# The sample's half of the last projection, from channels on the partitions to tokens on the partitions

## The chip, the core and the metric

The kernel runs on one core of one Trainium2 chip. The metric is the device time of one execution in microseconds (us), as the median of several runs. TensorE multiplies matrices, VectorE and ScalarE work on tiles of 128 partitions, SyncE (SP) issues most transfers and ScalarE's queue (ACT) some.

## The reference

A hybrid encoder layer: one big input projection, three branches (S5, GLA, RG-LRU), a gated sum of their outputs, an output projection, the residual and a final norm. There is one prompt of 512 tokens and one sample of 256; both go through the same layer with 2048 channels. What the change touches is the end:

```python
m = gates[:, :, 0] * (y_a @ w_out_a) + gates[:, :, 1] * (y_b @ w_out_b) + gates[:, :, 2] * (y_c @ w_out_c)
z = z + m @ w_o                                   # w_o: 2048 x 2048
y = z * rsqrt(mean(z * z, axis=-1) + 1e-6) * final_norm_g
```

Inputs and outputs are float32. Each operand is split into an upper and a lower part (hi, lo); a product is hi x hi + hi x lo + lo x hi, three matmuls.

## The kernel before

Tiles hold channels on the 128 partitions and tokens in the columns. Everything here happens in `merge_and_project`. Program order gives the order of each engine's instructions to a scheduler that may move them as far as the buffers allow; on the chip each engine runs its own fixed list.

The prompt's loop goes over eight pairs of column tiles of w_o (p), four steps each (sb). A step's weights come as four quarters B12, B11, B21, B22 in one load of 512 KB (`fetch`, `quarter_weights`, L1205 is the load). The tile `raw` has two buffers. ScalarE casts three of the quarters to `hi` (128x768, L88), VectorE subtracts to get `lo` (L60); `weight_sums` puts the four sums T1 to T4 into `t`, which has one buffer, with three VectorE instructions (`t<-raw` 128x512, then two of 128x256); then `t` is split the same way (128x1024). `hi` and `lo` have three buffers each, and a step takes two of each. `products` (L1144) runs seven products by Winograd's form, 42 matmuls of 256 columns per step: the products 1, 2 and 3 take the split quarters, then 6, 7, 5 and 4, of which the first three and the last take the split sums.

Behind the products of each step stand 12 matmuls of the sample (`sample_mm`, L1417): the quarters B11 and B21 are plain columns of w_o, so they serve as stationary weights while the sample's 256 tokens move. After four steps `combine` takes the seven products from PSUM and adds them to the residual (one ScalarE copy and 11 VectorE instructions of 128x256), and the sample's tile is added and written to the scratch tensor `zspill`. The squares of the prompt's previous pair (`square`) run on ScalarE and are summed on VectorE in the loop.

The tail does the sample's other eight column tiles: three loads per tile (`fetch_last`, 384 or 320 KB, L1472), their split, 48 matmuls of 256 columns (L1417). Between these splits stand the prompt's norm (`prompt_norm`, a matmul with a matrix of ones, L1493) and the 16 scalings and output transfers of the prompt (`prompt_out`). The sample's norm goes across partitions by a matmul with ones (L1542), and eight products of 128x512 with eight transfers of 256 KB end the kernel (L1548).

Of the kernel before, what the change touches and what calls it, by code (L numbers as in the profile page):

```python
# [30 lines left out]
PN = (1, 2)  # L31
# [63 lines left out]
def build(tc, A, out_p, out_s):  # L95
# [11 lines left out]
    zspill = drm.tile([8, 128, NS], F32, name="zspill")  # L107
    xnorm = drm.tile([16, 128, NT], F32, name="xnorm")

# [103 lines left out]
    def proj(ci, n0):  # L213
        """column tile ci of w_in against the activations; two PSUM banks of T/2 or NT/2 tokens"""
# [10 lines left out]
    def evac(dst, ps, n0, func=AF.Copy, scale=1.0):  # L225
        """dst (AP [128, T or NT]) = func(ps * scale)"""
# [14 lines left out]
    # merge tiles piecewise, between the steps of a branch that keeps the vector engine busy: rate microseconds of the  # L241
    # tensor engine for one of the vector engine
# [37 lines left out]
    def cover(n):  # L280
        """n steps"""
# [10 lines left out]
    def flush():  # L292
        """no tile is left half done"""
# [5 lines left out]
    # the first u tiles: two with the contraction outermost, so that they run while x arrives, and a third and the  # L299
    # low-rank gate before the norms are there  # L300
# [41 lines left out]
    # rows 0..31 carry the upper parts of the gate's weights, rows 32..63 the lower ones  # L342
# [6 lines left out]
    # u, cut into chunks of 8 tokens: ud[channel, token of the chunk, chunk]  # L349
# [20 lines left out]
    # the activations get their norm  # L370
# [37 lines left out]
def branch_s5(E):  # L408
# [4 lines left out]
    NG, L, NQ, NE = 32, 8, T // 8, 8     # groups, chunk, chunks, eighths of the groups  # L413
# [56 lines left out]
    # quadrant bits of n1: n1 = 4 m + 2 b2 + b1  # L470
# [22 lines left out]
    # f = (A - 1) / lambda  # L493
# [8 lines left out]
    TT(n1, n1, r, mul)                      # re f  # L502
# [26 lines left out]
    # A^8 for the rows of the scan: backwards twice, forwards twice  # L529
# [11 lines left out]
    def coef(tab, base, kstep, k0, nk):  # L541
        """[128, 4 groups, nk, 16] view of table entries, power k0 + kstep * slot"""
# [4 lines left out]
    # chunk inputs X = E^T U into W  # L547
# [54 lines left out]
    # outputs: within the chunk (T), from the states before it and after it  # L602
    def within(e):
# [3 lines left out]
        for d in range(2):  # L607
# [10 lines left out]
            # B with its factor f; the fifth group is only there to fill 32 columns  # L618
# [65 lines left out]
    # skip, gelu, glu, gate; tokens in the order (token of the chunk, chunk)  # L684
# [58 lines left out]
def branch_gla(E):  # L743
# [42 lines left out]
    for hp in range(2):  # L786
        # cumulated log gates, restarted in every block of 128 tokens
# [27 lines left out]
        # v by tokens: [token, block, (head of the pair, dv)], block 0 the meta tokens  # L815
# [19 lines left out]
        # states before each block  # L835
# [49 lines left out]
        # blocks  # L885
# [39 lines left out]
        # norm over dv, with the next projections between  # L925
# [28 lines left out]
def exp_acc(V, out, x, r, k, ki):  # L954
    """out = exp(x), to the last bits; 0 and inf outside of float32's range; r, k and ki are places for the parts"""
# [13 lines left out]
def lru_rates(V, col, cst, gp):  # L969
    # c = -8 softplus(-lam)  # L970
# [23 lines left out]
def branch_lru(E, first, cp, cn):  # L994
# [8 lines left out]
    def load_half(ci, hk):  # L1003
        """the weights run a half tile ahead"""
# [18 lines left out]
    def conv(n, ps):  # L1023
        """the convolution of channel tile n, and the weights of its gates"""
# [22 lines left out]
    # the functions of a pair of channel tiles by the tables that they need  # L1047
# [16 lines left out]
    def decays(n, gate):  # L1064
        out = []
        for d in range(2):
# [4 lines left out]
            # 1 - a^2 = tanh(-log a) (1 + a^2)  # L1071
# [55 lines left out]
def weight_sums(V, r, t):  # L1127
    """r: B12, B11, B21, B22; t: T1, T3, T2, T4"""
# [6 lines left out]
def products(PE, ps, ws, sb, n, operand, nt=HN):  # L1135
    """two of the n steps of the seven products' contraction, for nt tokens of either half"""
# [31 lines left out]
def merge_and_project(E, yh, yl, out_p, out_s):  # L1168
    """the sum of the gated branch outputs, its projection, the residual and the final norm, channels on the partitions.
    The third branch goes by Winograd's form, the others as they are, for some column tiles before it and for the rest  # L1170
    behind it. The projection of the prompt goes by Winograd's form too. The sample's goes as it is, with the weights
    that are there for the prompt for the first column tile of every pair, and behind the prompt for the second."""
# [13 lines left out]
    def slot(n, dt=F32):  # L1186
        """one of the 28 places of a tile of all tokens, m0 to m15 and c0 to c11"""
# [33 lines left out]
    def fetch():  # L1221
        """the weights of the step after those that are there"""
# [75 lines left out]
    def third(p):  # L1298
# [11 lines left out]
        for e in range(2):  # L1310
# [3 lines left out]
            else:  # L1314
                # no place is left for whole gates
# [35 lines left out]
    def whole(k):  # L1351
        """an operand that both the prompt and the sample take as it is"""
# [32 lines left out]
    def z_pieces(j):  # L1385
        """the place of a channel tile of the prompt's output: (AP, first token, tokens)"""
# [14 lines left out]
    rest = {}  # L1401

    def rest_tile():
        if not rest:
            rest["m7"] = slot("m7")
        return rest["m7"]

    def square(j, h):
        """the squares of half a channel tile, added to the sum"""
        sq, acc = z_tile(10)[:, ss], rest_tile()[:, h * HP:(h + 1) * HP]  # L1410
        S.activation(out=acc if j == 0 else sq, in_=z_halves(j)[h], func=AF.Square)
        return lambda: j and TT(acc, acc, sq, add)
# [6 lines left out]
    def sample_add(po, z):  # L1419
        TT(z, po[:, :NS], z, add)  # L1420

    zsp = E["zspill"]
    for p in range(8):
        ps = seven()
        po = next_bank()
        for sb in range(4):
            if p:
                later = square(2 * (p - 1) + sb // 2, sb % 2)
            ws = ahead.pop(0)
            products(PE, ps, ws, sb, 8, out_operand, HP)  # L1430
            for kk in range(2):
                for i in range(2):
                    # B11, then B21
                    sample_mm(po, [x[:, i] for x in ws[:2]], kk, 2 * sb + kk + 8 * i, sb == kk == i == 0,
                              sb == 3 and kk == i == 1)
            fetch()
            if p:
                later()
            if sb == 2:
                for j in (2 * p, 2 * p + 1):  # L1440
                    residual(j)
                zs = rest_tile()[:, ss]
# [348 lines left out]
```

## Time and profile before

| | |
|---|---|
| runs | 2052.61, 2052.55, 2051.8 us; median 2052.55 |
| profiled execution | span 2048.7 us from its first to its last instruction; no time of its own beside that is given, and the median lies 3.85 us above the span |
| TensorE, weight loads | 2012.0 us (98%), 1983.8 us (97%) |
| VectorE, ScalarE | 1477.2 us (72%), 798.3 us (39%) |
| prompt's loop | first product 1781.67, last sample matmuls end 1989.0 |
| tail | 1989.0 to 2035.5, then 13.3 us to the end |

A row of a timeline gives the start, the duration, the engine, the line and the operation as "written tile <- read tiles"; in brackets stands how long the engine was idle before it, and what released it. The duration of a matmul is longer than the distance to the next one, because they overlap; what a matmul costs in a stream is that distance. For VectorE too, the next instruction may start before the one ahead has ended. Granted clock 1.00 is 2.4 GHz.

### The profile page before, as it was taken

The page shows a single profiled execution, that of the slowest core. Times are in us where ns is not written, and L with a number is a line of the kernel's source. Part 1 is how long each engine was busy: PE and PEld are TensorE (multiplying, and loading weights), DVE is VectorE, ACT ScalarE, POOL GpSimd, SP SyncE. Part 2 cuts the span into 40 slices and gives each one's busy share as a digit, 9 for nine tenths or more (in the row PEclk, how much of TensorE's full clock was granted, in tenths as well). Part 3 has the DMA queues.
Part 4 walks back from the last instruction along what each step waited for, and adds up shares of the span by engine and source line. Part 5 has one row for each costly group of instructions (what it writes and reads, how often), then busy time and mean ns, then how long its engine had stood idle before and what let it go on. Part 6 is the DMA issues. An engine that isn't in the chain of part 4 may idle for free.

```text
span 2048.7 us, 30974 instructions
## 1 busy us (share of the span) xinstructions
PE 2012.0 (98%) x12276; PEld 1983.8 (97%) x12276; DVE 1477.2 (72%) x2738; ACT 798.3 (39%) x1162; POOL 0.2 (0%) x4
## 2 busy tenths in 40 slices
PE   8999989999999999999999999999999999999997
PEld 8999989999998999999999999999999999999997
DVE  8988982634565678687776566656668988887778
ACT  7332111423343677543333222222235435533345
POOL 0000000000000000000000000000000000000000
PEclk9999999999999999999999999999999999999999
DMA  8752134422011222253333222222256335532246
GB/s 291 253 119 95 73 100 126 143 74 74 33 69 40 68 77 75 91 195 124 134 134 111 88 103 103 103 88 103 103 173 223 124 105 182 173 126 93 93 160 219
DMA packets 104225, 248.97 MB, mean 122 GB/s; under 512 B 18832, under 2 KB 39824, under 8 KB 104080
## 3 DMA queue, kind: packets, MB, share of 16 engines
q1 hardware_dynamic: 76496, 199.04, 29.1%
q10 hardware_dynamic: 27584, 47.96, 6.6%
q8 instruction: 96, 1.57, 0.3%
q14 instruction: 49, 0.40, 0.1%
HBM read 199.07 MB, written 47.88 MB: 121 GB/s over the span
## 4 chain that ended last, share of the span: by engine, by line
PE 83%; DVE 10%; ACT 3%; DMA 2%; issue 1%; SPq 0%; ACTq 0%; DVEq 0%
PE br L1144 22%; PE pm L1144 21%; PE pm L198 16%; PE pm L272 8%; PE pm L1417 4%; DVE sc L60 2%; DMA c<-gspill 2%; DVE W L60 2%; PE pm L331 2%; DVE lo L60 1%; PE br L1287 1%; PE pm L1287 1%; PE br L1057 1%; DVE m L60 1%; PE br L198 1%; PE br L1417 1%
## 5 line engine op out<-in xcount | busy, mean ns | idle before, releaser
L88 ACT ACTIVATE hi<-raw 128x768 fp32r<-128x768 f32 (+2 forms) x234 | 217.6, 930 | 526.6 <-PE pm L198 135.2
L60 DVE TENSOR_TENSOR lo<-raw,hi 128x768 fp32r<-128x768 f32 (+2 forms) x234 | 248.1, 1061 | 168.5 <-ACT hi L88 168.4
L60 DVE TENSOR_TENSOR lo<-t,hi 128x1024 fp32r<-128x1024 f32 x132 | 161.6, 1224 | 184.0 <-ACT hi L88 183.8
L88 ACT ACTIVATE hi<-t 128x1024 fp32r<-128x1024 f32 x132 | 139.9, 1060 | 265.1 <-PE br L1144 133.8
L198 PE MATMUL pm<-h,hi 128*128 128x392 f32 (+1 forms) x736 | 195.8, 344 | 1.2 <-ACT xp L1026 1.2
L198 PE MATMUL pm<-h,lo 128*128 128x392 f32 (+1 forms) x736 | 192.4, 341 | 2.5 <-DVE lo L60 2.5
L198 PE MATMUL pm<-l,hi 128*128 128x392 f32 (+1 forms) x736 | 192.9, 341 | 0.0
L1144 PE MATMUL br<-l,hi 128*128 128x384 f32 (+1 forms) x592 | 189.1, 319 | 0.0
L1144 PE MATMUL br<-h,lo 128*128 128x384 f32 (+1 forms) x592 | 188.5, 318 | 0.0
L1144 PE MATMUL br<-h,hi 128*128 128x384 f32 (+1 forms) x592 | 188.5, 318 | 0.0
L1144 PE MATMUL pm<-l,hi 128*128 128x384 f32 (+1 forms) x464 | 153.5, 331 | 0.1
L1144 PE MATMUL pm<-h,lo 128*128 128x384 f32 (+1 forms) x464 | 152.4, 328 | 0.0
L1144 PE MATMUL pm<-h,hi 128*128 128x384 f32 (+1 forms) x464 | 152.4, 328 | 0.0
L198 PEld LDWEIGHTS pm<-h,lo 128*128 128x128 f32 x736 | 134.9, 188 | 2.8 <-DVE lo L60 2.8
L198 PEld LDWEIGHTS pm<-h,hi 128*128 128x128 f32 x736 | 134.9, 189 | 2.8 <-ACT xp L1026 1.5
L198 PEld LDWEIGHTS pm<-l,hi 128*128 128x128 f32 x736 | 134.4, 189 | 0.2
L272 PE MATMUL pm<-h,lo 128*128 128x384 f32 x512 | 131.2, 337 | 2.0 <-DVE lo L60 2.0
L272 PE MATMUL pm<-h,hi 128*128 128x384 f32 x512 | 133.1, 341 | 0.0
L272 PE MATMUL pm<-l,hi 128*128 128x384 f32 x512 | 131.8, 338 | 0.0
L1144 PEld LDWEIGHTS br<-h,lo 128*128 128x128 f32 x592 | 111.5, 188 | 0.0
L1144 PEld LDWEIGHTS br<-h,hi 128*128 128x128 f32 x592 | 111.2, 188 | 0.2 <-ACT h L88 0.2
L1144 PEld LDWEIGHTS br<-l,hi 128*128 128x128 f32 x592 | 111.2, 188 | 0.0
(361 smaller groups left out, 4681.0 us busy)
## 6 DMA issues: line engine op xcount, KB each, us to landing
raw<-in_w_st SPq DMA_DIRECT2D x84, 512.0 KB
raw<-in_w_in SPq DMA_DIRECT2D x82, 512.0 KB
gspill<-g ACTq DMA_DIRECT2D x48, 384.0 KB
raw<-in_w_ost SPq DMA_DIRECT2D x32, 512.0 KB
xr<-in_xT SPq DMA_DIRECT2D x31, 392.0 KB
m<-gspill SPq DMA_DIRECT2D x26, 384.0 KB
raw<-in_w_out SPq DMA_DIRECT2D x16, 512.0 KB
raw<-in_w_outc SPq DMA_DIRECT2D x16, 512.0 KB
```

What stands on the lines that cost most here:

```text
L60: return f(*a, **k)
L88: ins = self.eng.activation(**k)
L198: PE.matmul(ps[h][:, :nw], w[:, k, :], xx[kt][:, n0 + h * nw:n0 + (h + 1) * nw], start=(kt == 0 and j == 0), stop=(kt == 15 and j == 2))
L272: PE.matmul(ps[h][:, :HN], w[:, k % 8, :], xx[k][:, NM + h * HN:NM + (h + 1) * HN], start=(k == 0 and j == 0), stop=(k == 15 and j == 2))
L331: PE.matmul(ps0[2 * t + h][:, :HT], w[:, k, :], xx[kt][:, h * HT:(h + 1) * HT], start=(kt == 0 and j == 0), stop=(kt == 15 and j == 2))
L1057: PE.matmul(ps[:, :HC], w[:, gs], xx[:, sl], start=(j == 0), stop=(j == 2))
L1144: PE.matmul(ps[j][:, :nt], w[:, wi, kk, :], x, start=(k == 0 and q == 0), stop=(k == n - 1 and q == 2))
L1287: PE.matmul(ps[h][:, :HN], w[:, 4 * b + k, :], yy[4 * b + k][:, h * HN:(h + 1) * HN], start=(k == 0 and j == 0), stop=(k == 3 and j == 2))
L1417: PE.matmul(po[:, :NS], x[:, n, :], y[k][:, ss], start=(first and j == 0), stop=(last and j == 2))
```

## The change

The sample's matmuls leave the loop: a step has 42 matmuls. `zspill` is gone. After the loop the whole sample product is made in the tail with the operands' roles exchanged: 128 tokens of the sample are the stationary operand, 512 output columns of w_o move. The tail has four chunks of 512 columns (c), in each of them eight units (u) of two contraction tiles; a unit is a load of 512 KB, a split, and six matmuls of 512 columns for either half of the tokens (t = 0, 1). All of w_o is loaded a second time for it, 32 x 512 KB, into the two buffers of `raw`, the one of `t`, and two half tiles, in turn. The first units' loads are issued in the last pair of the loop.

The residual and the final gain for the tokens' layout are loaded from new inputs (`load_chunk`, 16 transfers on ScalarE's queue, 3 MB). The squares of the prompt leave the loop and run at two tiles per unit from the first unit; the prompt's norm and its outputs follow. The sample's sum of squares is made along the row by ScalarE (`accum_out`), one column per chunk, so that the norm is one number per partition; no matmul with ones is needed. In the last chunk the second half of the tokens runs one unit behind the first, so that the first half's norm and outputs run beside its last matmuls. The output of the sample is [256, 2048], in eight transfers of 256 KB.

```diff
-    def sample_mm(po, w, n, k, first, last):
-        hi, lo = w
-        for j, (x, y) in enumerate(((hi, mh), (hi, ml), (lo, mh))):
-            PE.matmul(po[:, :NS], x[:, n, :], y[k][:, ss], start=(first and j == 0), stop=(last and j == 2))
+    def load_unit():
+        c, u = units.pop(0)
+        n = raws[0]
+        raws[0] += 1
+        if n % 4 < 3:
+            r = (bp.tile([128, 2, 512], F32, name="t") if n % 4 == 2 else
+                 wp.tile([128, 2, 512], F32, name="raw", bufs=2))
+            SP.dma_start(r[:], A["w_os"][c, :, 2 * u:2 * u + 2, :])
...
+    def split_unit():
+        if loaded:
+            hi = wp.tile([128, 2, 512], F32R, name="hi")
+            lo = wp.tile([128, 2, 512], F32R, name="lo")
+            for kk, r in loaded.pop(0):
+                split(hi[:, kk], lo[:, kk], r)
+            wq.append((hi, lo))
     for p in range(8):
         ps = seven()
-        po = next_bank()
         for sb in range(4):
-            if p:
-                later = square(2 * (p - 1) + sb // 2, sb % 2)
             ws = ahead.pop(0)
             products(PE, ps, ws, sb, 8, out_operand, HP)
-            for kk in range(2):
-                for i in range(2):
-                    sample_mm(po, [x[:, i] for x in ws[:2]], kk, 2 * sb + kk + 8 * i, sb == kk == i == 0,
-                              sb == 3 and kk == i == 1)
             fetch()
-            if p:
-                later()
+            if p == 7 and sb > 0:
+                load_unit()
...
+        if p == 7:
+            split_unit()
         combine(V, S, ps, u2, u3, z_halves(2 * p), z_halves(2 * p + 1), u4)
-        sample_add(po, zs)
-        SP.dma_start(zsp[p], zs)
+    def load_chunk(c):
+        for t in range(2):
+            S.dma_start(zc[c][t][:, pp], A["xs"][t, :, c * 512:(c + 1) * 512])
+            S.dma_start(zc[c][t][:, ss], A["g_row"][:, c * 512 + t * NS:c * 512 + (t + 1) * NS].to_broadcast([128, NS]))
+    def chunk_done(c, t, po):
+        z = zc[c][t][:, pp]
+        TT(z, po[:], z, add)
+        sq = bu.tile([128, NT], F32, name="u")[:, pp]
+        S.activation(out=sq, in_=z, func=AF.Square, accum_out=s_(t, c))
+        if c < 3:
+            for h in range(2):
+                TT(z[:, h * NS:(h + 1) * NS], z[:, h * NS:(h + 1) * NS], zc[c][h][:, ss], mult)
...
+    def unit_mm(po, w, t, u):
+        for kk in range(2):
+            k = 2 * u + kk
+            ts = slice(NP_ + t * 128, NP_ + (t + 1) * 128)
+            for q, (x, y) in enumerate(((mh, w[0]), (ml, w[0]), (mh, w[1]))):
+                PE.matmul(po[:], x[k][:, ts], y[:, kk], start=(k == 0 and q == 0), stop=(k == 15 and q == 2))
+    for c in range(4):
+        po = [next_bank() for t in range(2)]
+        held = None
+        for u in range(8):
+            if c == 0 and u < 4:
+                load_chunk(u)
+            w = wq.pop(0)
+            unit_mm(po[0], w, 0, u)
+            if c < 3:
+                unit_mm(po[1], w, 1, u)
+            elif held:
+                unit_mm(po[1], held, 1, u - 1)
+            held = w
+            load_unit()
+            split_unit()
+            for j in range(2):
+                if n < 16:
+                    prompt_square(n)
+                    n += 1
+                    if n == 16:
+                        prompt_norm()
+                        break
+            else:
+                if n == 16 and outs:
+                    prompt_out(outs.pop(0))
+        if c == 3:
+            chunk_done(3, 0, po[0])
+            sample_out(0)
+            unit_mm(po[1], held, 1, 7)
+            chunk_done(3, 1, po[1])
+            sample_out(1)
+        else:
+            for t in range(2):
+                chunk_done(c, t, po[t])
```

How the change moves instructions is seen in the engines' fixed lists; a name such as c_16486 is a place in SBUF, m_16528 the tile `m7`, which before holds the sum of squares and the sample's place, u the scratch of combine, pm and br PSUM banks.

VectorE between the last step of one pair and the second step of the next, from one split of sums (`lo<-t,hi`) to the following one. Before:

```order
L60 TENSOR_TENSOR lo<-t,hi 128x1024
L60 TENSOR_TENSOR u<-br,u 128x256
L60 TENSOR_TENSOR m_16528<-pm,m_16528 128x256
L60 TENSOR_TENSOR m_17779<-m_17779,u 128x256
L60 TENSOR_TENSOR lo<-raw,hi 128x768
L60 TENSOR_TENSOR u<-u,br 128x256
L60 TENSOR_TENSOR t<-raw 128x512
L60 TENSOR_TENSOR m_17470<-m_17470,u 128x256
L60 TENSOR_TENSOR t<-raw,t 128x256
L60 TENSOR_TENSOR t<-t,raw 128x256
L60 TENSOR_TENSOR m_16528<-m_16528,m_16644 128x256
L60 TENSOR_TENSOR lo<-t,hi 128x1024
```

After, at the same place:

```order
L59 TENSOR_TENSOR lo<-t,hi 128x1024
L59 TENSOR_TENSOR u<-pm,u 128x256
L59 TENSOR_TENSOR lo<-raw,hi 128x768
L59 TENSOR_TENSOR m_17998<-m_17998,u 128x256
L59 TENSOR_TENSOR t<-raw 128x512
L59 TENSOR_TENSOR u<-pm,u 128x256
L59 TENSOR_TENSOR t<-raw,t 128x256
L59 TENSOR_TENSOR m_17998<-m_17998,u 128x256
L59 TENSOR_TENSOR t<-t,raw 128x256
L59 TENSOR_TENSOR u<-u,pm 128x256
L59 TENSOR_TENSOR m_17997<-m_17997,u 128x256
L59 TENSOR_TENSOR lo<-t,hi 128x1024
```

The sample's addition (`m_16528<-pm`) and the squares' sum are gone; of combine's instructions four stand ahead of the last sum of `t`, as before. In the round ahead of this one two of them do (`u<-pm,u` and `m_17997<-m_17997,u`), also as before.

VectorE in the tail, where the prompt's scalings (`SCALAR_TENSOR_TENSOR` with `small`) stand among the splits. Before:

```order
L60 TENSOR_TENSOR lo<-m_18997,hi 128x640
L60 SCALAR_TENSOR_TENSOR c_16524<-c_16524,small,m_18786 128x512
L60 SCALAR_TENSOR_TENSOR c_16525<-c_16525,small,m_18786 128x512
L60 SCALAR_TENSOR_TENSOR c_16524<-c_16524,small,m_18786 128x256
L60 SCALAR_TENSOR_TENSOR c_16525<-c_16525,small,m_18786 128x256
L60 TENSOR_TENSOR c_18778<-pm,c_18778 128x256
L60 SCALAR_TENSOR_TENSOR c_16855<-c_16855,small,m_18786 128x512
L60 TENSOR_TENSOR lo<-m_19020,hi 128x640
L60 TENSOR_TENSOR c_18784<-c_18784 128x256
L60 SCALAR_TENSOR_TENSOR m_16856<-m_16856,small,m_18786 128x512
L60 TENSOR_TENSOR lo<-m_19043,hi 128x768
L60 SCALAR_TENSOR_TENSOR c_16855<-c_16855,small,m_18786 128x256
```

After, the last of the scalings ahead of the split of unit 17 (the addition `c_18316<-pm` of chunk 1 and two scalings stand ahead of these rows, the split of unit 16 is nine rows above that addition):

```order
L59 SCALAR_TENSOR_TENSOR c_16486<-c_16486,small,m_18323 128x256
L59 SCALAR_TENSOR_TENSOR c_16487<-c_16487,small,m_18323 128x256
L59 SCALAR_TENSOR_TENSOR c_16759<-c_16759,small,m_18323 128x512
L59 SCALAR_TENSOR_TENSOR m_16760<-m_16760,small,m_18323 128x512
L59 SCALAR_TENSOR_TENSOR c_16759<-c_16759,small,m_18323 128x256
L59 SCALAR_TENSOR_TENSOR m_16760<-m_16760,small,m_18323 128x256
L59 SCALAR_TENSOR_TENSOR m_17253<-m_17253,small,m_18323 128x512
L59 SCALAR_TENSOR_TENSOR m_17254<-m_17254,small,m_18323 128x512
L59 TENSOR_TENSOR c_18316<-c_18316 128x256
L59 TENSOR_TENSOR c_18316<-c_18316,c_18317 128x256
L59 TENSOR_TENSOR c_18317<-pm,c_18317 128x512
L59 TENSOR_TENSOR lo<-raw,hi 128x1024
```

Before, a split follows after at most five scalings; after, ten scalings, the chunk's products and both its additions stand ahead of the next split.

ScalarE at the end of the loop; `in_xs` and `in_g_row` are the new inputs, `hi<-t` and `hi<-raw` casts of the last steps of the loop and of the first unit:

```order
L87 ACTIVATE hi<-t 128x1024
L87 ACTIVATE hi<-raw 128x768
L1464 DMA c_18316<-in_g_row 128x256
L1463 DMA c_18317<-in_xs 128x512
L1464 DMA c_18317<-in_g_row 128x256
L1463 DMA c_18319<-in_xs 128x512
L1463 DMA c_18318<-in_xs 128x512
L87 ACTIVATE hi<-t 128x1024
L1464 DMA c_18318<-in_g_row 128x256
L1464 DMA c_18319<-in_g_row 128x256
L1463 DMA c_18320<-in_xs 128x512
L1464 DMA c_18320<-in_g_row 128x256
```

Before there was no transfer on ScalarE's queue here; now 16 stand among the last casts of the loop, and each waits on ScalarE's queue for its place.

## Rows read from the trace of the kernel before

**Rows 1.** Page: busy time and instructions by engine, chain by engine

```profile
PE 2012.0 (98%) x12276; PEld 1983.8 (97%) x12276; DVE 1477.2 (72%) x2738; ACT 798.3 (39%) x1162; POOL 0.2 (0%) x4
...
PE 83%; DVE 10%; ACT 3%; DMA 2%; issue 1%; SPq 0%; ACTq 0%; DVEq 0%
```

**Rows 2.** Windows: length, busy PE PEld DVE ACT POOL, PEclk, DMA share, GB/s

```profile
1680.00:1760.00 80.00, 80.00 (x460) 80.00 (x460) 72.34 (x122) 37.85 (x51) 0.00 (x0) 1.00 0.48 157
...
1810.00:1980.00 170.00, 170.00 (x1434) 170.00 (x1433) 128.73 (x238) 62.13 (x85) 0.00 (x0) 1.00 0.30 101
...
1786.90:1812.00 25.10, 24.09 (x203) 24.09 (x204) 24.54 (x43) 12.16 (x16) 0.00 (x0) 1.00 0.61 197
...
2002.00:2034.00 32.00, 32.00 (x272) 31.99 (x271) 31.12 (x57) 21.38 (x39) 0.00 (x0) 1.00 0.76 257
```

**Rows 3.** Waits of PE, 1767 to 2049: total, times, longest

```profile
PE pm L1417 <- DVE c L60: 1.1, 1, 1.1
PE br L1542 <- ACT c L88: 0.5, 1, 0.5
PE pm L1144 <- DVE c L60: 0.4, 1, 0.4
```

**Rows 4.** Timeline of ScalarE in the loop: start, duration, instruction, idle before

```profile
1795.59 1.06 ACT L88 ACTIVATE hi<-t 128x1024 fp32r<-128x1024 f32 x1 [3.45 <-DVE t L60]
...
1872.07 1.06 ACT L88 ACTIVATE hi<-t 128x1024 fp32r<-128x1024 f32 x1 [3.26 <-PE br L1144]
```

**Rows 5.** Timeline of VectorE, a step in the middle of the loop

```profile
1873.16 1.23 DVE L60 TENSOR_TENSOR lo<-t,hi 128x1024 fp32r<-128x1024 f32 x1 [2.20 <-ACT hi L88]
1874.37 0.96 DVE L60 TENSOR_TENSOR lo<-raw,hi 128x768 fp32r<-128x768 f32 x1
1875.25 0.68 DVE L60 TENSOR_TENSOR t<-raw 128x512 f32<-128x512 f32 x1
1875.96 0.43 DVE L60 TENSOR_TENSOR t<-raw,t 128x256 f32<-128x256 f32 x1
1876.43 0.43 DVE L60 TENSOR_TENSOR t<-t,raw 128x256 f32<-128x256 f32 x1
```

**Rows 6.** Timeline of VectorE, first pair of the loop

```profile
1791.17 1.22 DVE L60 TENSOR_TENSOR lo<-t,hi 128x1024 fp32r<-128x1024 f32 x1
1792.31 0.95 DVE L60 TENSOR_TENSOR lo<-raw,hi 128x768 fp32r<-128x768 f32 x1
1793.18 0.69 DVE L60 TENSOR_TENSOR t<-raw 128x512 f32<-128x512 f32 x1
1793.78 0.68 DVE L60 TENSOR_TENSOR l<-m,h 128x512 fp32r<-128x512 f32 x1
...
1794.72 0.42 DVE L60 TENSOR_TENSOR u<-m,m 128x256 f32<-128x256 f32 x1
1795.05 0.42 DVE L60 TENSOR_TENSOR t<-t,raw 128x256 f32<-128x256 f32 x1
...
1802.71 1.23 DVE L60 TENSOR_TENSOR lo<-t,hi 128x1024 fp32r<-128x1024 f32 x1
```

**Rows 7.** Chain that ended last, pair 1: start, duration, matmuls

```profile
1814.43 1.43 PE pm L1417 x12
1815.86 0.71 PE pm L1144 x6
```

**Rows 8.** Timeline of VectorE in the tail, the prompt's scalings

```profile
2006.70 2.20 DVE L60 SCALAR_TENSOR_TENSOR c<-c,small,m 128x512 f32<-128x512 f32 x4
2008.82 0.41 DVE L60 TENSOR_TENSOR c<-pm,c 128x256 f32<-128x256 f32 x1
```

**Rows 9.** Timeline of the end: last sample matmul, output issues

```profile
2035.10 0.29 PE L1417 MATMUL pm<-h,lo 128*128 128x256 f32 x1
...
2040.83 3.99 ACTq L1548 DMA_DIRECT2D out<-c  x4
```

**Rows 10.** Waits of SP's queue, 1800 to 1990

```profile
SPq L1205 <- DVE t L60: 113.1, 25, 6.5
```

More of the change, by code (lines that the diff above doesn't have):

```diff
@@ L30 @@
 WH = 3
-PN = (1, 2)
 XS = 2
@@ L106, in build @@
     hspill = drm.tile([12, 128, NT], F32, name="hspill")
-    zspill = drm.tile([8, 128, NS], F32, name="zspill")
     xnorm = drm.tile([16, 128, NT], F32, name="xnorm")
@@ L1419, in sample_add @@
-    def sample_add(po, z):
-        TT(z, po[:, :NS], z, add)
-    zsp = E["zspill"]
+    units = [(c, u) for c in range(4) for u in range(8)]
+    raws, loaded, wq = [0], [], []
+    def load_unit():
+        if not units:
+            return
+        c, u = units.pop(0)
[5 more added lines that the diff above has]
+            SP.dma_start(r[:], A["w_os"][c, :, 2 * u:2 * u + 2, :])
+            loaded.append([(slice(0, 2), r[:])])
+        else:
+            two = []
+            for kk in range(2):
+                r = slot(f"m{n // 4 % 2 * 2 + kk}")[:, pp]
+                SP.dma_start(r, A["w_os"][c, :, 2 * u + kk, :])
+                two.append((kk, r))
+            loaded.append(two)
@@ L1450, in merge_and_project, with prompt_square @@
                         whole(k)
+        if p == 7:
+            split_unit()
         u2, u3, u4 = thirds()
         combine(V, S, ps, u2, u3, z_halves(2 * p), z_halves(2 * p + 1), u4)
-        sample_add(po, zs)
-        SP.dma_start(zsp[p], zs)
-    zs = [slot(f"c{p}") for p in range(8)]
-    c8, m5, m6, m7 = slot("c8"), slot("m5"), slot("m6"), rest_tile()
-    acc_s, sq_s = c8[:, 0:NS], c8[:, ss]
-    parts = [(0, 6), (6, 11), (11, 16)]
-    raws = []
-    def raw():
-        t = slot(f"m{len(raws) % 5}")
-        raws.append(t)
-        return t
-    def fetch_last(p, i):
-        k0, k1 = parts[i]
-        n = k1 - k0
-        r = raw()
-        SP.dma_start(r[:, :n * 128], A["w_os"][p, :, k0:k1, :])
-        return r, n
-    def split_last(r, n):
-        hi = wp.tile([128, 8, 128], F32R, name="hi")
-        lo = wp.tile([128, 8, 128], F32R, name="lo")
-        v = lambda t: t[:].rearrange("p k n -> p (k n)")[:, :n * 128]
-        split(v(hi), v(lo), r[:, :n * 128])
-        return hi, lo
+    zc = [[slot(f"c{2 * c + t}") for t in range(2)] for c in range(4)]
+    m5, m6, m7 = slot("m5"), slot("m6"), slot("m7")
+    st = m5[:, ss]
+    acc = m7[:, pp]
+    def load_chunk(c):
+        for t in range(2):
+            S.dma_start(zc[c][t][:, pp], A["xs"][t, :, c * 512:(c + 1) * 512])
+            S.dma_start(zc[c][t][:, ss], A["g_row"][:, c * 512 + t * NS:c * 512 + (t + 1) * NS].to_broadcast([128, NS]))
+    def prompt_square(j):
+        u = bu.tile([128, NT], F32, name="u")
+        for z, o, n in z_pieces(j):
+            S.activation(out=(acc if j == 0 else u)[:, o:o + n], in_=z, func=AF.Square)
+        if j:
+            TT(acc, acc, u[:, pp], add)
     def rstd(r, v, tmp, ps):
@@ L1492, in prompt_norm @@
         ps = next_bank()
-        PE.matmul(ps[:], E["ones"][:], m7[:, pp], start=True, stop=True)
-        rstd(m6[:, pp], m5[:, pp], m7[:, pp], ps[:])
+        PE.matmul(ps[:], E["ones"][:], acc, start=True, stop=True)
+        rstd(m6[:, pp], m5[:, pp], acc, ps[:])
     def prompt_out(j):
@@ L1499, in prompt_out @@
             SP.dma_start(out_p[j * 128:(j + 1) * 128, o:o + n], z)
-    def sample_square(p, e):
-        z = zs[p][:, e * NS:(e + 1) * NS]
-        first = p == e == 0
-        S.activation(out=acc_s if first else sq_s, in_=z, func=AF.Square)
-        if not first and p + e < 8:
-            TT(acc_s, acc_s, sq_s, add)
-        S.activation(out=z, in_=z, func=AF.Copy, scale=col("final_g", 2 * p + e))
-    steps = [(p, i) for p in range(8) for i in range(3)]
-    loads = [fetch_last(*s) for s in steps[:4]]
@@ L1541, in merge_and_project @@
-    for i, x in enumerate((acc_s, sq_s)):
-        PE.matmul(pr[:, :NS], E["ones"][:], x, start=(i == 0), stop=(i == 1))
-    r = m6[:, ss]
-    rstd(r, m5[:, ss], m7[:, ss], pr[:, :NS])
-    for p in range(8):
-        z = zs[p][:, pp].rearrange("p (e n) -> p e n", e=2)
-        TT(z, z, r.unsqueeze(1).to_broadcast([128, 2, NS]), mult)
-        (SP, S)[p % 2].dma_start(out_s[2 * p * 128:(2 * p + 2) * 128, :].rearrange("(e p) n -> p e n", p=128), z)
+    s_ = lambda t, i: st[:, 16 * t + i:16 * t + i + 1]
@@ new lines, in sample_out @@
+    def sample_out(t):
+        b, v, w, tmp, r = (s_(t, i) for i in range(4, 9))
+        S.activation(out=tmp, in_=s_(t, 3), func=AF.Ln, scale=1.0 / 2048, bias=b)
+        V.scalar_tensor_tensor(out=w, in0=s_(t, 3), scalar=-0.5 / 2048, in1=v, op0=mult, op1=add)
+        S.activation(out=r, in_=tmp, func=AF.Exp, scale=-0.5)
+        V.scalar_tensor_tensor(out=tmp, in0=r, scalar=w, in1=r, op0=mult, op1=mult)
+        V.scalar_tensor_tensor(out=r, in0=tmp, scalar=1.5, in1=r, op0=add, op1=mult)
+        rows = slice(t * 128, (t + 1) * 128)
+        for c in (0, 1, 2, 3):
+            z = zc[c][t][:, pp]
+            if c == 1:
+                S.activation(out=z, in_=z, func=AF.Copy, scale=r)
+            elif c < 3:
+                V.tensor_scalar(out=z, in0=z, scalar1=r, scalar2=None, op0=mult)
+            else:
+                for h in range(2):
+                    y = z[:, h * NS:(h + 1) * NS]
+                    V.scalar_tensor_tensor(out=y, in0=y, scalar=r, in1=zc[c][h][:, ss], op0=mult, op1=mult)
+            (S if c == 1 else SP).dma_start(out_s[rows, c * 512:(c + 1) * 512], z)
@@ L1789 @@
     out = r.results[0]
-    return tuple(np.ascontiguousarray(out[f"out_{i}"].transpose(0, 2, 1)) for i in range(2))
+    return np.ascontiguousarray(out["out_0"].transpose(0, 2, 1)), np.ascontiguousarray(out["out_1"])
```

55 lines of the change are left out of this document (14 added, 41 removed).

## The prediction

> **What bounds the kernel now.** I read the page first: TensorE is busy 98% of the span and the chain that ended last lies on it for 83% [rows 1]. I then cut the last 290 us into stretches. In the prompt's loop TensorE is never idle, at a granted clock of 1.00 (the 2.4 GHz level), while VectorE has a quarter of its time free; in the first pair of the loop VectorE is full (24.54 of 25.10 us), and in the tail nearly so (31.12 of 32), with the DMA engines at 0.76 [rows 2]. TensorE's waits behind the loop's start are three, 2.0 us together [rows 3]. So each matmul removed is worth its whole pitch, as long as ScalarE and VectorE can deliver weights at the new pace. That is the question of this change, and it is read from what paces them today: ScalarE's cast of the weight sums stands idle 3.26 us for TensorE before it starts [rows 4]. Today TensorE sets the pace.
>
> **Sum, part by part** (us; minus is a gain).
>
> *Matmuls of the loop.* 1434 matmuls of 256 columns take 170.00 us, 0.1186 each [rows 2]. 12 per step in 32 steps leave: 384 x 0.1186 = **-45.5**. A step falls from 54 matmuls, 6.41 us, to 42, 4.98 us; a pair from 25.6 to 19.92.
>
> *Matmuls of the tail.* Before 384 of 256 columns, 45.5. After 384 of 512 columns, a form the trace has not. Two rows bound it: 256 columns 0.1186, and 384 columns 80.00/460 = 0.1739 [rows 2]. Going on in a straight line gives 0.229; adding only the 0.0533 that 128 columns take at 2.4 GHz gives 0.227. I take 0.2298, the upper side, as the step from 256 to 384 was above that too. 384 x 0.2298 = 88.2, so **+42.7** (41.7 at the other end). The whole sample product thus falls by only 91.1 - 88.2 = 2.9. The page "TensorE: Matmul & The Clock Gate" of the Trainium skill, section "Wait — 56ns, not 53.3ns?", gives a fixed 2.5 ns above the columns' time per matmul: the tail would be 384 x 0.2157 = 82.8 and the result 5.4 lower. By that rule 256 columns are 0.1092; the trace does not agree, it has 9.4 ns more.
>
> *The weights' chain in the loop.* With half of each step's slack gone, this becomes the bound. VectorE's order is fixed, the sums' tile t has one buffer: split of t, split of raw, three sums into t, cast of t on ScalarE, next split of t. From start to start the trace shows 1.21, 0.88, 0.71, 0.47 [rows 5], then 0.54 to ScalarE's cast (1795.05 to 1795.59) and 1.09 to the next split (1872.07 to 1873.16) [rows 4 to 6]: 4.90 per step, just under the 4.98 of TensorE. But in every pair the 11 instructions of combine stand between two of these rounds. Their pitch is 0.33, and independent instructions follow at 1.14, 0.87 and 0.60 [rows 6]. By the order above, three short ones come before the last sum of t in the first round: 1.14+0.87+0.60+3x0.33+1.63 = 5.24; five more in the second: 1.14+0.87+0.60+5x0.33+1.63 = 5.89. A pair is 5.24+5.89+2x4.90 = 20.9 against 19.92: 1.0 lost, in six pairs **+6.0**. Today 25.6 covers it. Below: nothing lost, if the splits run a step ahead; above 1.5 a pair, 9.
>
> *The first pair.* VectorE still makes operands there and has no gap, so its work does not come earlier because TensorE has less. The first step's next split ends at 1791.17+1.22, when TensorE needs it [rows 6]. From the split at 1802.71 two rounds of the boundary kind lead to 1802.71+5.24+5.89+1.23 = 1815.1, when pair 1, step 1 has its second weights. Before, TensorE needs them 20 matmuls (2.4) behind the sample group that ends 1814.43+1.43 [rows 7], so at 1818.2. It gains 3.1 of the five groups' 7.1: **+4.0**. (The 1.1 wait [rows 3] goes too and is inside.) Bounds 2.5 to 5.
>
> *Into the tail.* The last steps' raw loads share two buffers and the SP queue with the first units, and ScalarE issues 16 loads between its casts. SP's queue waits 113 us for VectorE's sums to free raw, at no cost today [rows 10], as there was room. I take **+1.2**, 0 to 4.
>
> *VectorE in the tail.* Before, the prompt's scalings stand between the splits one to five at a time; after, ten are in a row ahead of unit 17's split (order above). Four took 2008.82 - 2006.70 = 2.12 [rows 8]; ten (six long, four short) are 2 x 2.12 + 1.41 = 5.65. With the addition ahead (0.60), the products (0.66), the other addition (0.60) and the split (1.22), 8.7 pass from the end of chunk 1's first half. TensorE has 1.38 of unit 15, 2.76 of unit 16 and two matmuls (0.46) to do: it waits 4.1, and 1.4 more as the norm's instructions just ahead end later. **+5.5** (4 to 6.5). The norm's matmul waits for the last sum of squares: **+0.6**. Afterwards VectorE needs at most 2.7 per unit against 2.76.
>
> *The end.* From the last sample matmul (2035.10) to the end of the span are 13.3, of which the eight products and their issues go to 2044.8 [rows 9]. After, half the output is already out, norms are single columns and the scaling is shorter: about 11.0, **-2.3** (-1 to -3.5).
>
> *At nothing:* the squares moved into the tail (ScalarE is at 67% there: 21.38 of 32), the spill of z (off the path), and the extra bytes: the tail moves about 26 MB in 95 us, some 275 GB/s, where 257 is a share of 0.76 [rows 2], so about 0.81. If that cover goes, it is rival 3.
>
> Sum: -45.5 + 42.7 + 6.0 + 4.0 + 1.2 + 5.5 + 0.6 - 2.3 = **+12.2**. The span of 2048.7 becomes 2060.9; the runs' median, 2052.55, lies 3.85 above the span, so 2064.8, said as 2065.
>
> **Rivals.**
> 1. *The chain keeps ahead (faster).* ScalarE's idle time [rows 4] is real room; if the cast of the next sums starts a step early and the tail's scalings end before unit 16 does, TensorE stays the bound: -45.5 + 42.7 - 2.3 = -5.1, so 2047.5. It decides at 19.92: the boundary rounds would have to fall from 11.1 to 10.1 us. For it: TensorE's three waits are small now. Against it: one buffer of t and a fixed order. Chance 0.12.
> 2. *Only one of the two binds.* Without the pair loss +6.2, 2058.8; without the burst and the norm's wait +6.1; without both and with the first pair +0.1. So 2053 to 2059. Chance 0.24.
> 3. *Transfers and queues.* The DMA page ("DMA: Bandwidth & Descriptors") of the Trainium skill, section "Anatomy of one DMA — SWDGE (gpsimd) path", says that a DMA's wait is served by the sequencer that issues it; SP's 113 us of waits agree [rows 10]. In the new order ScalarE's loads wait for places that TensorE frees, with casts queued behind them: if the last three steps and the first units each pay a round more, 6 to 8 is added: 2072. Against: the places of the first sums come free early. Chance 0.14.
> 4. *Wide matmuls overlap.* The same TensorE page, section "Back-to-back issue gap", has 131 ns for a stream of 512 columns with their weight loads. As a mechanism here: 512 columns would cost less than the 0.1739 of 384 [rows 2], the tail 50 and the result 38 lower, 2027. The rows grow with the columns, so chance 0.01.
>
> **How the numbers follow.** The forecast has 0.49. About 0.2%, 4.1 us, is what a measurement of this kernel can tell from no change. Faster takes most of rival 1 and rival 4: 0.12. Same takes the rest of 1 and the lower half of 2: 0.14. Slower is the rest, 0.74. All lower ends together are -45.5 + 41.7 + 0 + 2.5 + 0 + 4 + 0 - 3.5 = -0.8, 2051.8; all upper ends -45.5 + 42.7 + 9 + 5 + 4 + 6.5 + 1.2 - 1 = +21.9, 2074.5. Rival 1 lies below and rival 3 inside; the range of 8 in 10 is 2048 to 2075.
>
> **What would show it.** In the loop, TensorE's waits for VectorE's lo of t and ScalarE's hi of t, about 1 us once a pair, and a pair of 20.9; the loop's last matmul near 1953; in the tail a wait of 4 to 6 us at unit 17 behind ten scalings; 512 columns at 0.227 to 0.23. A loop at 19.92 a pair, or no wait at unit 17, would make the forecast wrong; idle TensorE with VectorE waiting for DMAs would be rival 3.

## The result

The changed kernel takes 2068.47 us (median of four runs, 2067.58 to 2070.61) where the kernel before takes 2052.18 (four runs): a ratio of 1.0084, 95% interval 1.0072 to 1.0096. It is slower by 16.3 us, where +12 was forecast.

The page of the changed kernel, busy time and chain, against [rows 1]:

```profile
PE 2023.5 (98%) x11888; PEld 1971.3 (95%) x11888; DVE 1492.3 (72%) x2739; ACT 802.6 (39%) x1155; POOL 0.2 (0%) x4
...
PE 80%; DVE 13%; ACT 3%; DMA 3%; issue 1%; ACTq 0%; DVEq 0%; SPq 0%
```

TensorE's busy time is up by 11.5 us and its idle time (the span less that) from 36.7 to 45.3. The spans of the two profiled executions differ by 20.1 us, more than the medians, and 4.9 of it lie ahead of the loop: there both kernels have the same instructions in the same order on every engine, but the loop's first product starts at 1786.55 in this execution (the slowest of the four) and at 1781.67 in the one of before. In the ten profiled executions of this study that moment lies between 1780.2 and 1786.6; what moves it was not tried. I therefore compare stages from the loop's first product on:

| stage (us) | before | after | difference | forecast |
|---|---|---|---|---|
| first product of the loop to first matmul of the tail | 207.2 | 175.9 | -31.3 | -34.3 |
| tail, to the start of its last matmul | 46.3 | 96.6 | +50.4 | +48.8 |
| from there to the end of the span | 13.6 | 9.8 | -3.8 | -2.3 |
| sum | 267.0 | 282.3 | +15.3 | +12.2 |

TensorE's waits from the loop to the end, against [rows 3]: three before, seven kinds now, 11.6 us together. The five longest:

```profile
PE br L1536 <- DVE lo L59: 4.3, 1, 4.3
PE br L1142 <- ACT hi L87: 3.8, 5, 2.4
PE pm L1142 <- ACT hi L87: 1.3, 4, 0.6
PE br L1142 <- DVE lo L59: 0.8, 2, 0.7
PE br L1142 <- DVE c L59: 0.7, 1, 0.7
```

The loop, timeline of VectorE, the splits of `t` across one pair; they answer to [rows 5], and a pair was 25.65 before:

```profile
1839.46 1.23 DVE L59 TENSOR_TENSOR lo<-t,hi 128x1024 fp32r<-128x1024 f32 x1 [0.41 <-ACT hi L87]
...
1844.28 1.23 DVE L59 TENSOR_TENSOR lo<-t,hi 128x1024 fp32r<-128x1024 f32 x1 [1.21 <-ACT hi L87]
...
1849.11 1.23 DVE L59 TENSOR_TENSOR lo<-t,hi 128x1024 fp32r<-128x1024 f32 x1 [1.21 <-ACT hi L87]
...
1854.45 1.21 DVE L59 TENSOR_TENSOR lo<-t,hi 128x1024 fp32r<-128x1024 f32 x1
...
1860.35 1.23 DVE L59 TENSOR_TENSOR lo<-t,hi 128x1024 fp32r<-128x1024 f32 x1 [0.41 <-ACT hi L87]
```

From 1839.46 to 1860.35 are 20.89 us, in steps of 4.82, 4.83, 5.34 and 5.90: the two plain rounds and the two at the pair's edge, as forecast (4.90, 4.90, 5.24, 5.89). The idle time in brackets is VectorE waiting for ScalarE's cast of `t`; three of the four casts in turn waited for VectorE's sums, not for TensorE any more as in [rows 4]. For the fourth (1859.26) the profile names TensorE, but it too starts 0.54 behind the start of the last sum, as the others do. One of the three, timeline of ScalarE:

```profile
1864.08 1.06 ACT L87 ACTIVATE hi<-t 128x1024 fp32r<-128x1024 f32 x1 [3.03 <-DVE t L59]
```

The end of the loop, chain of waits: the load of the last step's weights, from issue to landing, and the sums behind it.

```profile
1947.86 6.00 DMA raw<-in_w_ost
...
1953.95 0.70 DVE t L59
```

And TensorE in that place (windows: stretch, length, busy, clock, DMA share, GB/s):

```profile
1949.00:1952.00 3.00, 3.00 (x26) 1.00 1.02 369
1952.00:1954.80 2.80, 0.42 (x4) 1.00 0.93 333
1954.80:1957.00 2.20, 1.49 (x8) 0.88 0.91 318
1957.00:1959.00 2.00, 2.00 (x11) 0.50 0.79 228
1959.00:1960.60 1.60, 1.60 (x11) 0.72 0.58 145
1960.60:1963.00 2.40, 2.40 (x20) 1.00 0.77 273
```

A load that takes 6.00 us lets TensorE stand idle for 2.43 and then 0.66 us, with the DMA engines full; behind the idle time the clock falls to 0.50, the lower of the two levels (1.2 GHz).

The tail, timeline of VectorE around the run of scalings, against [rows 8]:

```profile
2007.34 0.68 DVE L59 TENSOR_TENSOR c<-pm,c 128x512 f32<-128x512 f32 x1
2007.94 2.86 DVE L59 SCALAR_TENSOR_TENSOR c<-c,small,m 128x512 f32<-128x512 f32 x5
...
2011.77 1.80 DVE L59 SCALAR_TENSOR_TENSOR m<-m,small,m 128x256 f32<-128x256 f32 x3
2013.49 0.42 DVE L59 TENSOR_TENSOR c<-c 128x256 f32<-128x256 f32 x1
...
2014.77 1.22 DVE L59 TENSOR_TENSOR lo<-raw,hi 128x1024 fp32r<-128x1024 f32 x1
```

Ten scalings (two of them in the rows left out) run from 2007.94 to 2013.49, 5.55 us; the split of unit 17 starts at 2014.77. TensorE's timeline at unit 17:

```profile
2016.04 0.79 PE L1536 MATMUL br<-lo,h 128*128 128x512 f32 x1 [4.25 <-DVE lo L59]
```

Its windows around that matmul:

```profile
2012.00:2016.00 4.00, 0.00 (x0) 0.81 0.82 301
2016.00:2018.00 2.00, 1.96 (x5) 0.50 0.44 78
2018.00:2020.00 2.00, 2.00 (x6) 0.50 1.19 339
2020.00:2022.00 2.00, 2.00 (x7) 0.66 0.66 178
2022.00:2024.00 2.00, 2.00 (x10) 1.00 1.02 390
```

It waits 4.25 us, and then 12 matmuls take 5.28 us, until 2021.32, at 0.44 instead of 0.23, so 2.5 more. Away from these places 512 columns cost 1.39/6 = 0.231 in a stream. The end, against [rows 9]: the last sample matmul, ScalarE's scaling and the last of its transfers.

```profile
2059.01 0.40 PE L1536 MATMUL pm<-lo,h 128*128 128x512 f32 x1
...
2063.24 0.72 ACT L87 ACTIVATE c<-c,m 128x512 f32<-128x512 f32 x1 [0.48 <-DVE m L59]
...
2063.99 0.35 ACTq L1529 DMA_DIRECT2D out<-c  x1
```

### The profile page after: what moved, and what is told of

It reads as the page before. It is cut to its first block, busy times and chain, and to the rows that moved or that the text cites. A ratio compares the mean times of both kernels' runs of the same rounds, so it can differ in the third digit from the quotient of the medians.

```text
span 2068.8 us, 30207 instructions
## 1 busy us (share of the span) xinstructions
PE 2023.5 (98%) x11888; PEld 1971.3 (95%) x11888; DVE 1492.3 (72%) x2739; ACT 802.6 (39%) x1155; POOL 0.2 (0%) x4
## 4 chain that ended last, share of the span: by engine, by line
PE 80%; DVE 13%; ACT 3%; DMA 3%; issue 1%; ACTq 0%; DVEq 0%; SPq 0%
PE br L1142 20%; PE pm L1142 20%; PE pm L196 16%; PE pm L270 5%; PE br L1285 3%; PE pm L1285 3%; PE pm L1536 2%; DVE sc L59 2%; DVE lo L59 2%; PE pm L329 2%; DVE W L59 2%; PE br L1536 2%; PE br L1055 1%; DVE m L59 1%; ACT hi L87 1%
## 5 line engine op out<-in xcount | busy, mean ns | idle before, releaser
L87 ACT ACTIVATE hi<-raw 128x768 fp32r<-128x768 f32 (+2 forms) x250 | 234.2, 937 | 544.7 <-PE pm L196 142.3
L59 DVE TENSOR_TENSOR lo<-raw,hi 128x768 fp32r<-128x768 f32 (+2 forms) x250 | 267.6, 1071 | 179.0 <-ACT hi L87 178.9
L1142 PE MATMUL br<-h,hi 128*128 128x384 f32 (+1 forms) x528 | 170.6, 324 | 3.5 <-ACT hi L87 2.4
L1142 PE MATMUL br<-l,hi 128*128 128x384 f32 (+1 forms) x528 | 171.3, 325 | 0.4 <-DVE l L59 0.4
L1142 PE MATMUL br<-h,lo 128*128 128x384 f32 (+1 forms) x528 | 170.7, 325 | 0.7 <-DVE lo L59 0.7
L1142 PE MATMUL pm<-l,hi 128*128 128x384 f32 (+1 forms) x528 | 171.1, 325 | 0.1
L1142 PE MATMUL pm<-h,lo 128*128 128x384 f32 (+1 forms) x528 | 170.4, 324 | 0.0
L1142 PE MATMUL pm<-h,hi 128*128 128x384 f32 (+1 forms) x528 | 170.0, 323 | 0.1
L1142 PEld LDWEIGHTS br<-h,hi 128*128 128x128 f32 x528 | 99.3, 188 | 4.3 <-ACT hi L87 2.6
L1142 PEld LDWEIGHTS br<-h,lo 128*128 128x128 f32 x528 | 99.7, 189 | 0.9 <-DVE lo L59 0.9
```

Source lines behind the costliest of these rows:

```text
L59: return f(*a, **k)
L87: ins = self.eng.activation(**k)
L1142: PE.matmul(ps[j][:, :nt], w[:, wi, kk, :], x, start=(k == 0 and q == 0), stop=(k == n - 1 and q == 2))
```

## The experiments

They ran beside a kernel before of 2051.0 us; the change's ratio puts the changed kernel at 2068.2 there. Three causes were to be told apart: the run of ten scalings, the loads at the end of the loop, and the chain through `t`. The rival in each case is one cause for all, too much work on VectorE or on the DMA engines.

**1. The scalings spread** (one tile per unit from unit 15):

```diff
-                if n == 16 and outs:
+                if n == 16 and outs and 8 * c + u >= 15:
                     prompt_out(outs.pop(0))
```

> The edit lets the prompt's scalings begin only with unit 15 of the tail, one tile per unit, so that two instead of ten stand ahead of the split of unit 17. Theory (the run of ten is the cause, and the idle time also costs clock): the 4.25 us wait of TensorE at unit 17 goes, and with it the 2016 to 2022 stretch at granted clock 0.50 to 0.66, worth another 2.5 us or so; the kernel falls by 6 to 7, from 2068.5 to about 2062. Rival A (VectorE has too much to do in the tail as a whole): the same work comes later, waits of the same sum appear at units 18 to 31, and the time stays within 2 us of 2068.5. Rival B (the wait alone counts, the clock falls for another reason): the fall is 4.25 and a stretch at 0.50 remains.

Measured: 2061.47 us, ratio to before 1.0046 (1.0031 to 1.0061). Windows of TensorE across unit 17, which now starts near 2006:

```profile
2005.00:2010.00 5.00, 5.00 (x23) 1.00 0.54 175
2010.00:2015.00 5.00, 5.00 (x23) 1.00 0.89 278
```

No wait is left in the tail and the clock stays at 1.00. Counted from the loop's first product, the span falls by 6.1, which is the 4.25 of waiting and most of the slow clock behind it; 512 columns cost 0.234 in this execution against 0.231, 1.2 over the whole tail, which the edit does not explain and which hides the rest. Rival A is out: the same scalings cost nothing where they stand apart. Rival B would have left the slow clock, some 2.5, behind; see run 6.

**2. The residual's loads behind the first units' casts** (`follow` orders a transfer behind ScalarE's last cast):

```diff
-            S.dma_start(zc[c][t][:, pp], A["xs"][t, :, c * 512:(c + 1) * 512])
+            S.follow(S.dma_start(zc[c][t][:, pp], A["xs"][t, :, c * 512:(c + 1) * 512]), S.last)
...
-            if c == 0 and u < 4:
-                load_chunk(u)
+            if c == 0 and 0 < u < 5:
+                load_chunk(u - 1)
```

(The gain's load is ordered the same way.)

> The edit issues the 16 loads of the sample's residual and gain on ScalarE's queue behind the first units' casts instead of in the last pair of the loop. Theory (3 MB share the DMA engines with the raw weights of the last step, whose load took 6.0 us from issue to landing): that load lands in 3 to 4 us, the waits of 2.43 and 0.66 us before the tail go together with the slow clock behind them, and the kernel falls by 3 to 5.5, from 2068.5 to about 2064. Rival A (the last step's load is late because the first unit's load took its buffer of raw): the load still is issued near the same place in the loop and the wait shrinks by less than 1 us. Rival B (loads moved into the tail delay the units' weights): a new wait for DMA appears in the first eight units.

Measured: 2067.08 us, 1.0071 (1.0056 to 1.0086). The last step's load in the chain of waits:

```profile
1946.21 3.19 DMA raw<-in_w_ost
```

TensorE's waits from 1940 on:

```profile
PE br L1536 <- DVE lo L59: 5.0, 1, 5.0
PE pm L1536 <- DVE lo L59: 0.8, 1, 0.8
PE pm L1536 <- ACT hi L87: 0.5, 1, 0.5
```

By the total this can't be told from the changed kernel (2068.2); by place both theory and rival B hold. The load takes 3.19 us instead of 6.00, the wait ahead of the tail is gone, and the last split of `t` in the loop comes 2.2 us earlier. But the 3 MB now meet the weights of the tail: two new waits, 0.8 and 0.5, in the ninth unit, whose chain of waits leads back to a load that takes long,

```profile
1967.18 6.55 DMA raw<-in_w_os
```

and a longer wait at unit 17 (5.0 for 4.25). Of some 4 us gained at the end of the loop 1.5 are left, counted from the loop's first product. Rival A is out: the last step's load is issued 161.2 us behind that product, in the changed kernel 161.3, and the wait is gone all the same.

**3. The sums into `t` ahead of the split of `raw`** in the prompt's loop (the edit shortened; `weight_sums` now returns its last instruction):

```diff
-        split(rh[:], rl[:], r[:, 1:4])
-        weight_sums(V, r, t)
+            S.activation(out=rh[:], in_=r[:, 1:4], func=AF.Copy)
+            last = weight_sums(V, r, t)
+            S.follow(TT(rl[:], r[:, 1:4], rh[:].bitcast(F32), sub), last)
```

> The edit puts the three sums into t ahead of the split of raw on VectorE in the prompt's loop, with the same instructions. Theory (a chain through the single buffer of t sets the loop's pace): the chain per step falls from 4.83 to about 4.0 and at the pair's edge from 11.2 to about 9.4, TensorE paces the loop, a pair falls from 20.89 to 19.92 and the kernel by about 6, from 2068.5 to about 2062.5. Rival (VectorE's amount of work sets the pace, some 18 of 20.9 us a pair, or the loads of raw): the order of the same instructions does not matter, a pair stays at 20.5 to 20.9 and the time within 1.5 us of 2068.5.

Measured: 2058.78 us, 1.0036 (1.0023 to 1.0048). VectorE in the middle of the loop, the splits of `t` across one pair:

```profile
1871.75 1.23 DVE L59 TENSOR_TENSOR lo<-t,hi 128x1024 fp32r<-128x1024 f32 x1
...
1881.72 1.23 DVE L59 TENSOR_TENSOR lo<-t,hi 128x1024 fp32r<-128x1024 f32 x1 [1.25 <-ACT hi L87]
...
1891.70 1.23 DVE L59 TENSOR_TENSOR lo<-t,hi 128x1024 fp32r<-128x1024 f32 x1
```

A pair is 19.95 us: TensorE sets the pace again, with no wait in the six pairs. The instructions are the same ones, so VectorE's amount of work was not the limit; the rival is out. The gain, 9.4, is above the 6 that was expected: counted from the loop's first product the loop is 9.9 shorter. The six pairs give 5.9 of it, as expected; 4.5 come behind them, in the last steps, where the load of raw is now issued earlier (see run 7); the first pair gives nothing (32.5 us for 32.05 up to pair 1, step 1's second weights).

**4. All three edits.**

> All three edits together. Theory (three separate causes that add): 2068.5 - 6.5 - 4.5 - 6 = 2051.5, range 2049 to 2055, thus level with the kernel before (2052.2); TensorE without a wait of over 1 us from the loop's first pair to the last matmul. Rival (one cause behind them, VectorE's or the DMA engines' total load): the parts do not add, the time stays above 2058.

Measured: 2053.80 us, 1.0008 (0.9998 to 1.0017). From the loop's first product to the end it is 267.5 us, level with before (267.0), and 14.7 below the changed kernel; the three parts, measured in the same way, are 6.1, 1.5 and 10.0, so the sum of 17.7 is not quite reached. TensorE's waits from 1940 on:

```profile
PE pm L1541 <- ACT hi L87: 1.5, 2, 1.3
```

1.5 us of waiting for ScalarE's casts at the start of the tail, where the deferred loads meet the weights.

**5. The same order of sums in the kernel before.** The edit is that of run 3.

> The kernel before, with the sums into t put ahead of the split of raw in the prompt's loop, as in the run that did so in the changed kernel and gained about 9. Theory (the chain through t binds only when a pair of TensorE takes less than 20.9 us): before, a pair takes 25.65 us of TensorE, so the edit is worth nothing there, within 1.5 us of the kernel before. Rival (the edit is good in itself, by fewer waits on VectorE or ScalarE anywhere): the kernel before also falls by 4 us or more.

Measured: 2050.50 us, 1.0002 (0.9993 to 1.0012). Nothing, as the theory has it: 6.41 us of TensorE per step covered the chain before. So it is the shorter step that made the chain the bound.

**6. The wait filled with work that nobody uses.** 18 added matmuls ahead of unit 17; the product is unchanged.

```diff
+            if (c, u) == (2, 0):
+                pd = next_bank()
+                for i in range(18):
+                    PE.matmul(pd[:], mh[i % 16][:, NP_:NP_ + 128], w[0][:, i % 2], start=True, stop=True)
             held = w
```

> The changed kernel with 18 matmuls of 512 columns, whose result nobody reads, in the place where TensorE waits 4.25 us ahead of unit 17's third matmul; they take 18 x 0.231 = 4.16 us and add nothing to the product. The wait for the split stays as it is. Theory (idle TensorE loses its clock and pays again behind the wait): the stretch at granted clock 0.50 to 0.66 behind the wait goes, the kernel falls by 2 to 3 us, from 2068.5 to 2066. Rival (the slow clock has another reason, or the wait alone costs): the time stays, or rises by up to 4 if the added matmuls come on top of the wait.

Measured: 2067.56 us, 1.0081 (1.0067 to 1.0094), level with the changed kernel within the intervals. The windows behind the filled wait:

```profile
2014.00:2016.00 2.00, 1.92 (x9) 1.00 0.31 45
2016.00:2018.00 2.00, 2.00 (x9) 1.00 0.83 316
2018.00:2020.00 2.00, 2.00 (x10) 1.00 0.69 144
```

The clock stays at 1.00. From the end of unit 16 to the start of the 18th matmul of the product behind it are 8.76 us against 10.87 in the changed kernel, so the slow clock was worth 2.1 in that place, as the theory has it, and rival B of run 1 is out. The median shows only 0.6 of it, which is what the rival expected of the total: in this execution 512 columns cost 0.234 to 0.235 each against 0.231, which is 1.0 over the rest of the tail, and the loop took 0.5 longer; for neither have I a cause. The total is thus inconclusive, the place is not.

**7. Scalings spread and sums ahead, the loads as in the change.**

> The scalings spread and the sums ahead, without the deferred loads. Theory (deferring the 3 MB moved the contention into the first units, where it cost 2 to 3 us, and with the sums ahead the last step's load is issued early enough): 2068.2 - 7 - 9.5 = 2051.7, level with or 1 to 2 us below the run with all three edits (2053.8). Rival (the deferred loads were needed): the wait of 2 to 3 us ahead of the tail is back, and the time is 2 to 4 above that run.

Measured: 2051.19 us, 1.0005 (0.9996 to 1.0014). The ratio can't be told from run 4's; from the loop's first product on it is 266.0, 1.6 less than run 4, and of the waits at the end of the loop one of 0.52 us is left. The last step's load still takes long beside the 3 MB, but it is issued 8.9 us earlier, counted from the loop's first product, than in the changed kernel:

```profile
1935.25 5.50 DMA raw<-in_w_ost
```

The deferred loads were not needed once the sums came first; the rival is out.

**8. As run 7, each chunk's residual loaded in the middle of its own chunk** (ordered by `follow` as in run 2):

```diff
-            if c == 0 and u < 4:
-                load_chunk(u)
+            if u == 4:
+                load_chunk(c)
```

> As the run before this one, with each chunk's residual and gain loaded in the middle of its own chunk (0.75 MB at unit 4 of each), so that no 3 MB burst meets the weights anywhere. Theory (the contention of transfers is what is left at the end of the loop and the start of the tail): no wait of TensorE above 0.5 us from the last pair to the end, 2049 to 2051, level with the kernel before or up to 2 us faster. Rival (what is left is VectorE's and ScalarE's order there): within 1 us of the run before this one.

Measured: 2050.94 us, 0.9999 (0.9990 to 1.0008). TensorE's waits from the loop's first product to the end:

```profile
PE pm L1142 <- DVE lo L59: 2.2, 2, 1.4
PE br L1142 <- DVE c L59: 0.7, 1, 0.7
PE br L1142 <- ACT hi L87: 0.4, 1, 0.4
```

All come before 1813, in the first pair and the two steps behind it; the theory's wait-free tail is there. From the loop's first product to the end of the span it is 263.8 us against 267.0 before, 3.2 less, and 2.2 less than run 7. The loads explain of these 2.2 the 0.8 at the end of the loop; 1.1 are the price of 512 columns, 0.231 to 0.233 in this execution and 0.234 in that of run 7, with no wait in either tail. By the medians the rival (within 1 us of run 7) holds as well: 2050.94 and 2051.19 can't be told apart. Nor do the medians show the 3.2: its loop began at 1783.1, the one of before at 1781.7. Whether the part ahead of the loop is really later in the changed kernels (1782.7 to 1786.6 in eight executions against 1780.2 and 1781.7 in two of the old form), with the same instructions, is open.

## Why the prediction was right

The sign, the places and most sizes came out; the measured +16.3 lies within the range and above the forecast of +12.

- **Matmuls.** 512 columns take 0.231, forecast 0.2298; the tail's stream is 88.8 instead of 88.2. The rule of the Trainium skill ("TensorE: Matmul & The Clock Gate", "Wait — 56ns, not 53.3ns?") gives 0.2157, by estimate 82.8 for the tail; the trace has 15 ns more per matmul, and the measurement decides. The 131 ns of the same page of the Trainium skill ("Back-to-back issue gap", rival 4) do not show here. So the turn saves TensorE 91.1 - 88.8 = 2.3 us, and that is all that it can save there.
- **The chain through `t`.** 20.89 a pair for the forecast 20.9; over six pairs 1818.60 to 1944.19 is 125.6, as worked out. Runs 3 and 5 show the cause. TensorE shows it less plainly than was forecast: of the 1.0 a pair only 0.2 is listed as idle, the rest are delays of 0.1 to 0.14 at several matmuls and the like, which the overlap of matmuls hides.
- **The first pair.** TensorE reaches pair 1, step 1's second weights 32.05 after the loop's start, before 36.15: it gains 4.1 where 3.1 was forecast, so the term was 3.0 and not 4.0.
- **Into the tail: the term that was mis-sized.** Forecast +1.2, at most 4; measured 5.4. From the last wait of the six pairs (1944.19) to the tail's first matmul (1962.40) TensorE needs 24 matmuls and two steps, 12.8, and took 18.2. I had counted places and queues, and not that 3 MB of residual (333 to 369 GB/s in all) share the DMA engines with the one load that the chain waits for (6.00 us against 3.19, run 2), nor that this load is issued too late to hide it (run 7). The sign that was named for rival 3 came, idle TensorE behind a transfer, but not its mechanism, casts queued behind ScalarE's loads: ScalarE's cast of that step starts at 1953.96, 0.10 behind the landing, beside VectorE's sum. And behind 3.1 of waiting came some 1.7 of slow clock (each window's length times the clock that it lacks); about half of the last 0.6 is that idle time is counted from the end of a matmul's record, 0.28 behind its start, where the next would have started after 0.12; the rest I can't place.
- **The run of scalings.** Wait forecast 5.5 (4 to 6.5), measured 4.25; but it costs 2.1 (run 6) to 2.5 (the 12 slow matmuls) more by the clock, which I had left out altogether. Together 6.4 to 6.8, and run 1 returns 6.1 by stage and 6.7 by the medians. The norm (+0.6) cost about 0.3: TensorE's weight load for it waits 0.4, and the gap that it makes in the stream is 1.1 where it was 0.9.
- **The end.** -3.8 for -2.3 (the prediction's 13.3 counts from the end of the last sample matmul, the table's 13.6 from its start): one number per partition saves more than I gave it, the first half's addition and norm run beside the last matmuls, and ScalarE's last transfer is issued 5.0 us after the start of the last matmul (2059.01 to 2063.99), where before the issues of the four transfers on that queue went on to 2044.8, 9.7 behind it [rows 9].
- **Luck.** The misses went both ways: 4.2 too little into the tail and 2.5 for the clock left out, against 1.0 too much for the first pair, 1.2 for the wait at unit 17 and 1.5 for the end. That the sum came within 3 us (from the loop's first product on) is in part luck; the two largest costs, the loop's chain and the wait at unit 17, are not.
- Rivals: 1 did not occur, since both waits were there. 2 is what run 1 or run 3 alone makes, 2061 and 2059 (forecast 2053 to 2059). Faster than before was only to be had by taking the waits away, and even then (run 8) it is level.

## What to carry to other kernels

Work that is taken from the busiest engine is only worth what the engines that feed it can follow: before moving 1.43 us out of a step of 6.41, add up the serial round through every single-buffered tile from start to start; here it was 4.9 to 5.9 against the new 4.98, and putting three sums ahead of one subtraction was worth more (9.4 us) than the turn saves TensorE (2.3). Read the engines' fixed lists for runs of one kind of instruction ahead of something urgent, and spread them. A burst of loads that nobody needs soon should not meet the one load that everybody waits for: issue that load early enough (run 7) or spread the burst thin (run 8), rather than push it as a block to the next stage (run 2).

## What the runs showed of the hardware that I had not expected

Idle TensorE pays twice. Behind 2.43 us of idle time at the end of the loop and behind 4.25 at unit 17 the granted clock fell to 0.50 (1.2 GHz), at a cost of some 1.7 and 2.1 to 2.5 us; with the second gap filled by 18 useless matmuls it stayed at 1.00. The price is not fixed: in run 3 the wait at unit 17 is 4.16 us, and behind it only 7 matmuls are slow (2003.45 to 2006.60), 1.5 us, and the clock is back sooner (window from 2004 to 2008):

```profile
2004.00:2008.00 4.00, 4.00 (x13) 0.68 0.84 218
```

The waits of 0.2 us in each pair of the loop left it at 1.00 (1840 to 1900), and so did one of 1.37 us in run 8 (at 1807.57).

The price of the same 512-column stream at clock 1.00 differed between executions, 0.231 to 0.236 us, and within one (run 3: 0.236 at the start of the tail, 0.232 at its end); no run shows why, and over 384 matmuls it moves a stage by more than 1 us. And the 1780 us ahead of the loop, the same instructions in every kernel, differed by up to 6 us between the ten executions; a change of 0.2% is therefore read from its own stages, and even there a difference of 1 us between single executions shows little.
